# A transformer block with retention and top-k attention on one core: the last head's norm moved one block earlier and read from PSUM, and the last output weights split by converting and adding DMAs

## The chip, the cores and the metric

One NeuronCore of a Trainium2 chip runs the whole program; the other cores are idle. The metric is the device time of one execution in microseconds, median of three runs. Work is issued on five engines, each with its own queue: TensorE (PE, with its weight loads as PEld), VectorE (DVE), ScalarE (ACT), GpSimd (POOL) and SyncE (SP). DMAs are issued from SP, ACT or POOL queues.

## The reference

Layer input `h` has 16 meta tokens and 512 real ones (T = 528), width 1024, all in float32:

```
h = h + 0.5 * swiglu(rmsnorm(h), ffn1)          # width 2816
u = rmsnorm(h);  proj = u @ w_in                 # 11,848 columns: rq rk rv rg aq ak av iq ik iw g_ret g_att
yr = retention(rope(rq), rope(rk)/16, rv)        # 4 heads, dk 256, dv 512, decay per head
yr = yr * rsqrt(mean(yr*yr over dv) + eps)       # the head norm that the change moves
yr = (silu(rg) * yr) @ w_ret_out                 # 2048 x 1024: "output weights"
ya = top-k attention(rope(aq), rope(ak), av, index scores) @ w_att_out      # 8 heads, 128 keys kept
h = h + (sigmoid(g_ret) * yr + sigmoid(g_att) * ya) @ w_mix_out
h = h + 0.5 * swiglu(rmsnorm(h), ffn2);  return rmsnorm(h)
```

## The kernel before

Every float32 operand is kept as two fp32r parts, an upper one (the value rounded) and a lower one (the rest), and a product is three matmuls for each 128 x 128 weight tile: upper x upper, upper x lower, lower x upper (`mm3`). Tokens are the moving operand (512 or 2 x 264 columns), weights the stationary one.

The projections of the mixer run through one software pipeline, `steps_through` (L293). A step is (start of the load, source, product). In the block of step i it issues, in this order: the load of step i+4, the upper part of step i+2's weights, the product of step i with small jobs hung between its k tiles (`between`), the lower part of step i+2's weights, and what is to be done with the result (`behind`). Inside `manual_schedule(engines=BUSY)` PE, ACT and DVE issue in exactly the order in which the program emits them. SP and POOL are not in that list: their order is a planner's.

Raw weights land in a ring of two tiles (`raw`, 8 KB per partition each); a tile is free again when its last reader is done. The split parts lie in rings of three (`whi`, `wlo`). A step's weights are split in one of two ways: `in_two` (ACT rounds, DVE subtracts), or, for the last head's four output steps and one gate (the word "dma" in `how`), `in_two_by_dma`: ACT rounds into `whi`, ACT writes minus the rounded value into `wlo`, and a POOL DMA adds the raw tile onto `wlo` inside SBUF.

The end of the pipeline, which the change touches, runs these blocks (p = 3 is the last retention head):

- gr0 and gr1: two gates. `last_0` and `last_1` follow their products: ACT sigmoid, `weigh` (values times decayed scores, gate and squares), and in `last_1` two rounds of `pick` (`select_steps`: DVE takes the 8 largest index scores and blanks them).
- ak: keys of attention head 0. `norm_sums(p)` hangs before its k = 4: PE sums the squares, DVE scales them, POOL takes the power -0.5. `last_2`: `norm_diag` (DVE spreads the factors on a diagonal, ACT and DVE split it), then the keys' rope.
- aq: queries of head 0. `norm_all` hangs before its k = 3: two matmuls with ones spread the factors over the partitions, and ACT copies them from PSUM to SBUF (`rn`). `last_3`: `two_normed_parts` twice (DVE multiplies, ACT rounds, DVE subtracts, for the four 128-row parts of the head), then the queries' rope.
- ro0 to ro3: `outputs(p)`, four steps of the last head's output weights, 24 matmuls of 512 columns each; ro0 takes parts 0 and 1 first. Beside each: two rounds of `pick`, and DVE adds the results onto `accr`.
- gr4: a gate whose weights are split in the "dma" way; then the rest of the picks.

After the pipeline the attention stage begins: gate gr5 (`w = gr.next()`, L1948; an ordinary split, `split_w`, L117 and L118) and heads 0 to 7: scores, softmax, next head's projections, transposes. Head 0's mask for keys 128 to 255 (`bias`, L1291) comes from the last pick.

A rope (`rope_swap`) is two ACT copies that swap halves, three DVE operations, and a split.

Of the kernel before, what the change touches and what calls it, by code (L numbers as in the profile page):

```python
# [11 lines left out]
F32 = mybir.dt.float32  # L12
F32R = mybir.dt.float32r
AF = mybir.ActivationFunctionType
ALU = mybir.AluOpType
# [3 lines left out]
P = 128  # L19
D = 1024  # L20
KD = D // P
S = 512
NM = 16
T = S + NM
TX = 576
WPAD = 64
# [4 lines left out]
RH = 4  # L31
# [50 lines left out]
def kernel(ctx: ExitStack, tc: tile.TileContext, x, meta, g1, wg1, wu1, wd1, gm,  # L82
# [199 lines left out]
        nc.scalar.activation(hi, src, AF.Copy)  # L282
        return lambda: nc.vector.tensor_tensor(lo, src, hi.bitcast(F32), ALU.subtract)  # L283

    def in_two_by_dma(src, hi, lo):

        nc.scalar.activation(hi, src, AF.Copy)
        nc.scalar.activation(lo, src, AF.Copy, scale=-1.0)
        return lambda: nc.gpsimd.dma_start(lo, src, accum_op=ALU.add)

    BUSY = {mybir.EngineType.PE, mybir.EngineType.Activation, mybir.EngineType.DVE}

    def steps_through(steps):  # L293


        ws = {}

        def pre(i):
            if i < len(steps):
                steps[i][0]()  # L300

        def upper(i):
            if i < len(steps):
                v = steps[i][1]()
                n, c = v.shape[1:]
                at = (*steps[i], w_at[0])[3]
                hi, lo = (wpool.tile([P, 1024 + WPAD], F32R, tag=t, name=t, bufs=3)[:, at : at + n * c]
                          .rearrange("p (k c) -> p k c", k=n) for t in ("whi", "wlo"))
                ws[i] = (hi, lo, (in_two, in_two_by_dma)[len(steps[i]) > 4](v, hi, lo))

        def lower(i):
            if i < len(steps):
                ws[i][2]()

        for i in range(4):
            pre(i)
        for i in range(2):
            upper(i)
            yield
            lower(i)  # L320
            yield
        i = 0
        while i < len(steps):
            pre(i + 4)
            upper(i + 2)
            steps[i][2](ws.pop(i)[:2], lambda: lower(i + 2))
            yield
            i += 1
# [1025 lines left out]
    if True:  # L1354
# [152 lines left out]
        def norm_sums(h):  # L1507

            d = heads[h]
            col = sm_tile("psn")  # L1510
            for b in range(4):
                nc.tensor.matmul(col[:, b : b + 1], d["ssum"][:, b * P : (b + 1) * P], ones, start=True, stop=True)
            ms = rt.tile([P, 5], F32, tag="ms", name="ms", bufs=2)
            nc.vector.tensor_scalar(ms[:, :4], col[:, :4], 1.0 / DV, EPS, ALU.mult, ALU.add)
            r = d["rcol"] = rt.tile([P, 5], F32, tag="rcol", name="rcol", bufs=2)
            nc.gpsimd.tensor_tensor(r[:, :4], ms[:, :4], mhalf[:, :4], ALU.pow)

        def norm_diag(h):

            d = heads[h]  # L1520
            diag = tmp()[:, :S]
            d["diag"] = hi, lo = [tmp()[:, :S].bitcast(F32R) for _ in range(2)]
            TT(diag.rearrange("p (b c) -> p b c", b=4), ident.unsqueeze(1).to_broadcast([P, 4, P]),
               d["rcol"][:, :4].unsqueeze(2).to_broadcast([P, 4, P]), ALU.mult)
            return in_two(diag, hi, lo)

        def norm_all(h):

            d = heads[h]
            ps = sm_tile("psn")  # L1530
            for i, part in enumerate(d["diag"]):
                nc.tensor.matmul(ps, ones_r, part, start=i == 0, stop=i == 1)
            nc.scalar.activation(d["rn"], ps, AF.Copy)

        def normed_parts(h, c):

# [6 lines left out]
        def two_normed_parts(h, c):  # L1543
            lows = [normed_parts(h, c + i) for i in range(2)]
            for low in lows:
                low()


        raws = {}

        def tiles(key, src, c0, n, nk=KD, width=P):

            def one(i):
                def pre():
                    if i % 2 == 0:
                        m = min(2, n - i) * width
                        raws[key, i] = load_w(src[: nk * P, c0 + i * width : c0 + i * width + m], nk, m)
                return pre, lambda: raws[key, i // 2 * 2][:, :, i % 2 * width : (i % 2 + 1) * width]
            return [one(i) for i in range(n)]
# [3 lines left out]
        def pick(n):  # L1563

            for _ in range(n):
                next(picks["steps"], None)
# [5 lines left out]
        def proj(name, sl, between, behind):  # L1572

            def run(w, lower):
                if sl is None:
                    outs, ps = halves(mm_tile(name))
                else:
                    ps = sm_tile(name)
                    outs = [(ps, sl)]
                mm3(outs, w, xs, KD, between=between)  # L1580
                lower()
                behind(ps)
            return run

        def steps_of(tiles_, runs, *how):
            return [(*t, r, 0, *how) for t, r in zip(tiles_, runs)]

        THREE = ((2, pair), (4, pair), (7, pair))

# [95 lines left out]
        def outputs(h, beside):  # L1685

            def step(i):
                def run(w, lower):
                    if h == 0 and i == 0:
                        ixs.close()  # L1690
                        ap = accs.enter_context(pool("acc", 1, side="right"))
                        acc_r.extend(ap.tile([P, S], F32, tag=f"accr{c}", name=f"accr{c}") for c in range(KD))
                        vr["pool"] = vrs.enter_context(pool("vraw", 1, side="right"))
                    if i == 0:
                        if h + 1 < RH:
                            new_decay(h + 1)
                            place_tails(h + 1)
                        if h + 1 < RH:
                            heads[h + 1]["raw"] = fetch_values(h + 1, vraw())
                    pss = [sm_tile("psro") for _ in range(2)]  # L1700
                    rounds = [(j, 0, 4) for j in range(2)] if i else [(j, k, k + 2) for k in (0, 2) for j in range(2)]
                    for n, (j, k0, k1) in enumerate(rounds):
                        ps = pss[j]
                        mm3([(ps, slice(0, S))], [t[:, k0:k1, j * P : (j + 1) * P] for t in w],
                            lambda k: heads[h]["o"][k0 + k], k1 - k0, k0 == 0, True, k0 > 0)
                        if n == 0:
                            lower()
                            beside(i)
                        if k1 < 4:
                            continue  # L1710
                        a = acc_r[2 * i + j]
                        if h == 0:
                            nc.scalar.activation(a, ps, AF.Copy)
                        else:
                            TT(a, ps, a, ALU.add)
                    if i == 3 and h + 1 < RH:
                        decayed(h + 1)
                        if h + 2 == RH:
                            attention_tables()
                        values_in(h + 1)  # L1720
                return run

            how = ("dma",) if h + 1 == RH else ()
            return steps_of(tiles(("ro", h), w_ro[h * DV : (h + 1) * DV, :], 0, 4, DV // P, 2 * P),
                            [step(i) for i in range(4)], *how)

        def beside_outputs(h):
            def beside(i):
# [17 lines left out]
        def first_rope(ps, cols, n, parts):  # L1746

            y = rope_swap(ps, att["cos"][:, cols], att["sin"][:, cols], 64, n, nc.vector)
            return in_two(y, *parts)
# [13 lines left out]
        def last_1(ps):  # L1763
            keep_gate(ps)
            weigh(p, 3)
            pick(2)

        def last_2(ps):
            norm_diag(p)()
            first_rope(ps, slice(0, T), T, att["k"])()  # L1770

        def last_3(ps):
            two_normed_parts(p, 0)
            two_normed_parts(p, 2)
            first_rope(ps, REAL, S, att["q"])()

        more = gates_of(0)
# [2 lines left out]
            n = 4 - (h == p)  # L1780
            more += queries_keys(h) + gates[:n] + outputs(h - 1, beside_outputs(h - 1)) + gates[n:]
        more += steps_of(tiles("gr", w_in, OFF_GR + 2 * P, 2), [proj("psgate", REAL, (), last_0), proj("psgate", REAL, (), last_1)])
        more += steps_of(tiles("ak", w_in, OFF_AK, 1), [proj("psak", None, ((4, lambda: norm_sums(p)),), last_2)])
        more += steps_of(tiles("aq", w_in, OFF_AQ, 1), [proj("psaq", REAL, ((3, lambda: norm_all(p)),), last_3)])
        def beside_last(i):
            if i == 2:
                for c, t in enumerate(last_gates, 2):
# [1 line left out]
            pick(2)  # L1789

        more += outputs(p, beside_last)
        more += steps_of(tiles("gr4", w_in, OFF_GR + 4 * P, 1), [proj("psgate", REAL, (), first_kq.append)], "dma")
        steps += more
        with tc.manual_schedule(engines=BUSY):
            for _ in range(4):
# [486 lines left out]
```

## Time and profile before

| | |
|---|---|
| median of 3 runs | 1532.23 us (1531.75 to 1534.35) |
| profiled execution | 1531.78 us, of which its span 1530.0 us |
| PE busy | 1515.7 us, 99% of the span, 9791 matmuls |
| PEld, DVE, ACT, POOL busy | 1369.0, 1083.9, 730.8, 108.7 us |
| mean granted TensorE clock | 0.998 |
| DMA | 178.22 MB, mean 116 GB/s |

Times inside the execution count from the start of the span. "Idle before" is what an engine waited just ahead of an instruction, and the arrow names what ended the wait. A matmul's own duration overlaps its neighbours', so the pace is read from the distance between starts.

### The profile page before, as it was taken

What the parts mean: (1) busy time and instruction counts of PE and PEld (TensorE: products, weight loads), DVE (VectorE), ACT (ScalarE), POOL (GpSimd) and SP (SyncE); (2) the same over time, 40 slices, a digit from 0 to 9 for tenths busy, and PEclk for the clock granted to TensorE, in tenths of its full rate; (3) what the DMA queues carried; (4) which work ended last, traced back from release to release, by engine and by line L of the source; (5) the groups of instructions that cost most, each with busy time, mean ns of one, the idle gap of its engine ahead of it and who ended that gap; (6) DMA issues with size and microseconds to landing.
All of it is one profiled execution on the core that took longest, in us unless ns stands there. A gap on an engine that the chain in (4) does not pass through costs nothing.

```text
span 1530.0 us, 23979 instructions
## 1 busy us (share of the span) xinstructions
PE 1515.7 (99%) x9791; PEld 1369.0 (89%) x9791; DVE 1083.9 (71%) x1678; ACT 730.8 (48%) x1142; POOL 108.7 (7%) x142
## 2 busy tenths in 40 slices
PE   9999999999999999999999999999999999999998
PEld 8999999999888888788888788998888899899996
DVE  4987585776887767776858687666455788586675
ACT  6555353454354444443333447666335446254453
POOL 1000000003110120000000121111002000000000
PEclk9999999999999999999999999999999999999999
DMA  5232333326553453241312393233433322233232
GB/s 167 69 124 88 108 102 101 102 93 216 170 189 140 152 180 107 102 132 58 122 63 92 100 226 91 77 86 111 159 131 108 106 80 96 101 110 111 83 120 87
DMA packets 153390, 178.22 MB, mean 116 GB/s; under 512 B 5120, under 2 KB 124568, under 8 KB 152384
## 3 DMA queue, kind: packets, MB, share of 16 engines
q1 hardware_dynamic: 141968, 150.03, 30.2%
q0 software_dynamic: 6768, 18.20, 4.2%
q10 hardware_dynamic: 4544, 8.46, 1.6%
q8 instruction: 77, 1.26, 0.3%
q14 instruction: 33, 0.27, 0.1%
HBM read 158.04 MB, written 16.01 MB: 114 GB/s over the span
## 4 chain that ended last, share of the span: by engine, by line
PE 94%; issue 3%; DMA 1%; DVE 1%; POOL 1%; ACT 0%; POOLq 0%; ACTq 0%; SPq 0%
PE psqX L157 14%; PE psd L157 8%; PE psd L2116 8%; PE psqY L157 7%; PE psrg L157 6%; PE psro L157 4%; PE psvX L1139 4%; PE psqZ L157 3%; PE psrk L157 3%; PE psu L157 3%; PE psrq L157 3%; PE psga L157 3%; PE psmo L157 3%; PE psat L157 3%; PE psak L157 3%
## 5 line engine op out<-in xcount | busy, mean ns | idle before, releaser
L283 DVE TENSOR_TENSOR wlo<-raw,whi 128x1024 fp32r<-128x1024 f32 (+2 forms) x179 | 191.2, 1071 | 48.3 <-ACT whi L282 48.2
L282 ACT ACTIVATE whi<-raw 128x1024 fp32r<-128x1024 f32 (+2 forms) x179 | 164.5, 920 | 116.9 <-PE psd L157 37.6
L157 PE MATMUL psqX<-th,whi 128*128 128x264 f32 (+1 forms) x432 | 122.3, 283 | 0.0
L157 PE MATMUL psqX<-tl,whi 128*128 128x264 f32 (+1 forms) x432 | 122.3, 283 | 0.0
L157 PE MATMUL psqX<-th,wlo 128*128 128x264 f32 (+1 forms) x432 | 122.2, 283 | 0.0
L118 DVE TENSOR_TENSOR wlo<-raw,whi 128x1024 fp32r<-128x1024 f32 (+1 forms) x60 | 73.4, 1223 | 57.1 <-ACT whi L117 57.1
L282 ACT ACTIVATE whi<-wsum 128x1024 fp32r<-128x1024 f32 x72 | 76.3, 1060 | 70.7 <-PE psd L2116 22.0
L117 ACT ACTIVATE whi<-raw 128x1024 fp32r<-128x1024 f32 (+1 forms) x60 | 62.6, 1044 | 98.9 <-PE psat L157 26.4
L283 DVE TENSOR_TENSOR wlo<-wsum,whi 128x1024 fp32r<-128x1024 f32 x72 | 87.9, 1222 | 12.5 <-ACT whi L282 12.5
L157 PE MATMUL psro<-vo,whi 128*128 128x512 f32 x256 | 80.9, 397 | 2.9 <-ACT vo L282 2.7
L157 PEld LDWEIGHTS psqX<-th,whi 128*128 128x128 f32 x432 | 82.1, 190 | 0.1
L157 PEld LDWEIGHTS psqX<-tl,whi 128*128 128x128 f32 x432 | 82.0, 190 | 0.0
L157 PEld LDWEIGHTS psqX<-th,wlo 128*128 128x128 f32 x432 | 82.0, 190 | 0.0
L157 PE MATMUL psd<-hl,whi 128*128 128x264 f32 x352 | 71.3, 284 | 0.0
L157 PE MATMUL psd<-hh,wlo 128*128 128x264 f32 x352 | 70.7, 283 | 0.0
L157 PE MATMUL psd<-hh,whi 128*128 128x264 f32 x352 | 70.7, 282 | 0.0
L2116 PE MATMUL psd<-wlo,hh 128*128 128x512 f32 (+1 forms) x180 | 69.2, 384 | 0.0
L2116 PE MATMUL psd<-whi,hh 128*128 128x512 f32 (+1 forms) x180 | 69.2, 384 | 0.0
L2116 PE MATMUL psd<-whi,hl 128*128 128x512 f32 (+1 forms) x180 | 69.2, 384 | 0.0
L157 PEld LDWEIGHTS psro<-vo,whi 128*128 128x128 f32 x256 | 48.8, 191 | 14.7 <-ACT vo L282 3.1
L157 PEld LDWEIGHTS psd<-hh,wlo 128*128 128x128 f32 x352 | 54.4, 188 | 0.0
L157 PEld LDWEIGHTS psd<-hh,whi 128*128 128x128 f32 x352 | 54.1, 188 | 0.0
(459 smaller groups left out, 4529.1 us busy)
## 6 DMA issues: line engine op xcount, KB each, us to landing
raw<-in_ffn_w_up_dram SPq DMA_DIRECT2D x22, 1024.0 KB, 5.0
raw<-in_ffn_w_gate_dram SPq DMA_DIRECT2D x21, 1024.0 KB, 5.0
raw<-in_w_in_dram SPq DMA_DIRECT2D x19, 1024.0 KB, 5.0
raw<-in_w_in_dram SPq DMA_DIRECT2D x31, 512.0 KB, 3.5
raw<-in_ffn_w_down_dram SPq DMA_DIRECT2D x24, 512.0 KB, 4.2
w<-in_w_in_dram SPq DMA_DIRECT2D x24, 512.0 KB, 6.2
raw<-in_ffn_w_down_dram SPq DMA_DIRECT2D x12, 768.0 KB, 4.3
raw<-in_w_ret_out_dram SPq DMA_DIRECT2D x8, 1024.0 KB, 4.8
```

The costliest lines, as they stand in the source:

```text
L117: nc.scalar.activation(hi, src, AF.Copy)
L118: eng.tensor_tensor(lo, src, hi.bitcast(F32), ALU.subtract)
L157: nc.tensor.matmul(o, a[:, k, :], b[:, sl], start=first and k == 0 and i == 0, stop=last and k == nk - 1 and i == 2, skip_group_check=onto)
L282: nc.scalar.activation(hi, src, AF.Copy)
L283: return lambda: nc.vector.tensor_tensor(lo, src, hi.bitcast(F32), ALU.subtract)
L1139: nc.tensor.matmul(d[bank_][t], a, b[:, k, :], start=not onto and j + k + m == 0, stop=j + k == 3 and m == 2, skip_group_check=onto)
L2116: nc.tensor.matmul(ps, a[:, bs], m[:, j, :], start=first and i == 0, stop=last and i == 2, skip_group_check=onto)
```

## The change

Three things. First, the spread norm factors of heads 1 to 3 stay in PSUM: DVE multiplies with them there, and the ACT copy is left out (head 0 keeps it). Second, for the last head the norm's steps move up: `norm_sums` to ak's k = 3; one of the two picks of `last_1` moves into `last_2`, between the diagonal and its lower part; `norm_all` to aq's k = 1; the four normed parts from behind aq's product into it (k = 2 and k = 3); and the keys' rope from behind ak to behind aq, just ahead of the queries' rope. Third, the weights of ro0 to ro3 and gr4 come in a new way, `tiles_by_dma`: a POOL DMA loads them from DRAM and converts them to fp32r on the way (the raw tile itself is now the upper part, so `whi` isn't written), ACT writes minus that into `wlo`, and a second POOL DMA adds the same weights from DRAM.

```diff
         def upper(i):
             if i < len(steps):
                 v = steps[i][1]()
+                if isinstance(v, tuple):
+                    ws[i] = v
+                    return
...
-                ws[i] = (hi, lo, (in_two, in_two_by_dma)[len(steps[i]) > 4](v, hi, lo))
+                ws[i] = (hi, lo, in_two(v, hi, lo))
...
             for i, part in enumerate(d["diag"]):
                 nc.tensor.matmul(ps, ones_r, part, start=i == 0, stop=i == 1)
-            nc.scalar.activation(d["rn"], ps, AF.Copy)
+            if h:
+                d["rn"] = ps
+            else:
+                nc.scalar.activation(d["rn"], ps, AF.Copy)
...
+        def tiles_by_dma(src, c0, n, nk=KD, width=P):
+            raws_ = {}
+            def one(i):
+                def rows(c, m):
+                    return src[: nk * P, c0 + c : c0 + c + m].rearrange("(k p) c -> p k c", p=P)
+                def pre():
+                    if i % 2 == 0:
+                        m = min(2, n - i) * width
+                        raw = wpool.tile([P, 2048], F32, tag="raw", name="raw", bufs=2)
+                        raws_[i] = raw[:, : nk * m].bitcast(F32R).rearrange("p (k c) -> p k c", k=nk)
+                        nc.gpsimd.dma_start(raws_[i], rows(i * width, m))
+                def parts():
+                    hi = raws_[i // 2 * 2][:, :, i % 2 * width : (i % 2 + 1) * width]
+                    lo = wpool.tile([P, 1024 + WPAD], F32R, tag="wlo", name="wlo", bufs=3)[:, : nk * width]
+                    lo = lo.rearrange("p (k c) -> p k c", k=nk)
+                    nc.scalar.activation(lo, hi.bitcast(F32), AF.Copy, scale=-1.0)
+                    return hi, lo, lambda: nc.gpsimd.dma_start(lo, rows(i * width, width), accum_op=ALU.add)
+                return pre, parts
+            return [one(i) for i in range(n)]
...
         def last_1(ps):
             keep_gate(ps)
             weigh(p, 3)
-            pick(2)
+            pick(1)
         def last_2(ps):
-            norm_diag(p)()
-            first_rope(ps, slice(0, T), T, att["k"])()
+            first_kq.append(ps)
+            low = norm_diag(p)
+            pick(1)
+            low()
         def last_3(ps):
-            two_normed_parts(p, 0)
-            two_normed_parts(p, 2)
+            first_rope(first_kq.pop(), slice(0, T), T, att["k"])()
             first_rope(ps, REAL, S, att["q"])()
...
-        more += steps_of(tiles("ak", w_in, OFF_AK, 1), [proj("psak", None, ((4, lambda: norm_sums(p)),), last_2)])
-        more += steps_of(tiles("aq", w_in, OFF_AQ, 1), [proj("psaq", REAL, ((3, lambda: norm_all(p)),), last_3)])
+        more += steps_of(tiles("ak", w_in, OFF_AK, 1), [proj("psak", None, ((3, lambda: norm_sums(p)),), last_2)])
+        more += steps_of(tiles("aq", w_in, OFF_AQ, 1), [proj("psaq", REAL, ((1, lambda: norm_all(p)), (2, lambda: two_normed_parts(p, 0)),
+                                                                                  (3, lambda: two_normed_parts(p, 2))), last_3)])
...
-        more += steps_of(tiles("gr4", w_in, OFF_GR + 4 * P, 1), [proj("psgate", REAL, (), first_kq.append)], "dma")
+        more += steps_of(tiles_by_dma(w_in, OFF_GR + 4 * P, 1), [proj("psgate", REAL, (), first_kq.append)])
```

In `outputs` the last head takes `tiles_by_dma(w, 0, 4, DV // P, 2 * P)` in place of `tiles(("ro", h), ...)` in the same way: one load for ro0 and ro1, one for ro2 and ro3.

## Rows read from the trace of the kernel before

**Rows 1.** PE's waits over the whole span: total us, times, longest us.
```profile
PE psro L157 <- ACT vo L282: 2.7, 1, 2.7
PE psS L1907 <- ACT gate L1340: 1.1, 1, 1.1
```
**Rows 2.** PE in order of time, aq to gr4: start, us, instruction, idle before.
```profile
859.14 0.40 PE L157 MATMUL psaq<-xh,whi 128*128 128x512 f32 x1
...
861.22 0.62 PE L1532 MATMUL psn<-tmp,ones_r 128*128 128x512 f32 x2
...
864.87 0.39 PE L157 MATMUL psaq<-xh,wlo 128*128 128x512 f32 x1
...
867.94 0.50 PE L157 MATMUL psro<-vo,whi 128*128 128x512 f32 x1 [2.68 <-ACT vo L282]
...
882.30 0.50 PE L157 MATMUL psro<-vo,wlo 128*128 128x512 f32 x1 [0.55 <-DMA wlo<-raw]
...
892.95 0.39 PE L157 MATMUL psgate<-xh,whi 128*128 128x512 f32 x1
```
**Rows 3.** The chain that ended last: head 0's output steps; the last head's sums.
```profile
645.99 21.97 PE psro L157 x96
...
855.51 0.79 PE psn L1512 x8
```
**Rows 4.** Two stretches: us, PE, PEld, DVE, ACT, POOL busy, granted clock, DMA.
```profile
868.00:873.00 5.00, 4.78 (x13) 3.56 (x14) 4.38 (x8) 2.91 (x5) 0.00 (x0) 0.66 0.74 120
928.00:930.00 2.00, 0.87 (x7) 0.67 (x6) 1.70 (x5) 1.97 (x3) 0.43 (x1) 1.00 0.02 5
```
**Rows 5.** DVE in order of time, from the norm's sums to the queries' rope.
```profile
855.83 0.56 DVE L1288 MAX8 top<-score 128x8 f32<-128x384 f32 x1
...
856.97 0.15 DVE L1514 TENSOR_SCALAR ms<-psn 128x4 f32<-128x4 f32 x1
...
859.99 0.69 DVE L283 TENSOR_TENSOR tmp<-tmp 128x512 fp32r<-128x512 f32 x1 [0.70 <-ACT tmp L282]
861.24 0.71 DVE L1252 TENSOR_TENSOR tmp<-psak,cos 128x528 f32<-128x528 f32 x1 [0.56 <-ACT tmp L1251]
...
864.02 0.71 DVE L283 TENSOR_TENSOR akq<-tmp,akq 128x528 fp32r<-128x528 f32 x1 [0.71 <-ACT akq L282]
866.53 1.30 DVE L1538 TENSOR_TENSOR to<-to,three 128x512 f32<-128x512 f32 x2 [1.81 <-ACT three L1533]
...
870.52 1.29 DVE L283 TENSOR_TENSOR vo<-to,vo 128x512 fp32r<-128x512 f32 x2
872.34 0.69 DVE L1252 TENSOR_TENSOR tmp<-psaq,cos 128x512 f32<-128x512 f32 x1 [0.53 <-ACT tmp L1251]
...
875.05 0.69 DVE L283 TENSOR_TENSOR akq<-tmp,akq 128x512 fp32r<-128x512 f32 x1 [0.70 <-ACT akq L282]
```
**Rows 6.** POOL in order of time.
```profile
856.14 1.35 POOL L289 DMA_DIRECT2D wlo<-raw  x1 [65.57 <-ACT wlo L288]
857.28 1.29 POOL L1516 TENSOR_TENSOR rcol<-ms,mhalf 128x4 f32<-128x4 f32 x1
...
877.21 1.27 POOL L289 DMA_DIRECT2D wlo<-raw  x1 [9.72 <-ACT wlo L288]
```
**Rows 7.** ACT in order of time: the minus copy of ro2.
```profile
875.87 1.04 ACT L288 ACTIVATE wlo<-raw 128x1024 fp32r<-128x1024 f32 x1
```
**Rows 8.** Landing times, 850 to 900 (`wlo`), 850 to 960 (`vo`: converting and adding, 1 MB).
```profile
DMA to landing us min/median/max: 5.0/5.1/6.2
...
DMA to landing us min/median/max: 6.6/8.3/10.1
```
**Rows 9.** The chain that ended last, 850 to 955: gr5's load.
```profile
885.42 5.10 DMA raw<-in_w_in_dram
```
**Rows 10.** DVE in the attention stage's first microseconds.
```profile
891.72 1.23 DVE L118 TENSOR_TENSOR wlo<-raw,whi 128x1024 fp32r<-128x1024 f32 x1 [3.04 <-ACT whi L117]
...
912.83 0.29 DVE L1291 TENSOR_SCALAR bias<-score 128x256 f32<-128x256 f32 x1
```

More of the change, by code (lines that the diff above doesn't have):

```diff
@@ L283, in in_two @@
         return lambda: nc.vector.tensor_tensor(lo, src, hi.bitcast(F32), ALU.subtract)
[L285 to L289, printed above, removed]
     BUSY = {mybir.EngineType.PE, mybir.EngineType.Activation, mybir.EngineType.DVE}
@@ L1583, in proj, with steps_of @@
             return run
-        def steps_of(tiles_, runs, *how):
-            return [(*t, r, 0, *how) for t, r in zip(tiles_, runs)]
+        def steps_of(tiles_, runs):
+            return [(*t, r, 0) for t, r in zip(tiles_, runs)]
         THREE = ((2, pair), (4, pair), (7, pair))
@@ L1721, in step @@
                 return run
-            how = ("dma",) if h + 1 == RH else ()
-            return steps_of(tiles(("ro", h), w_ro[h * DV : (h + 1) * DV, :], 0, 4, DV // P, 2 * P),
-                            [step(i) for i in range(4)], *how)
+            w = w_ro[h * DV : (h + 1) * DV, :]
+            ts = tiles_by_dma(w, 0, 4, DV // P, 2 * P) if h + 1 == RH else tiles(("ro", h), w, 0, 4, DV // P, 2 * P)
+            return steps_of(ts, [step(i) for i in range(4)])
         def beside_outputs(h):
```

## The prediction

> **What bounds the kernel now.** I read the page first: PE is busy 99% of the span, so only what PE waits for, or runs at a lower clock, can be won. The list of PE's waits comes next. Its two long entries lie at the seam between the retention heads and attention: 2.7 us before the last head's output product, ended by ACT's split of the normed parts, and 1.1 us in head 1's scores [rows 1]. The other entries that name an output product, 0.5 and 0.2 us, lie in ro2 and ro0 too, none with heads 0 to 2, so the copies that heads 1 and 2 lose were not waited for.
>
> PE's timeline through the seam gives what is to be won [rows 2]. From the last start in aq (864.87) to the first in gr4 (892.95) are 28.08 us. The same 96 matmuls took 21.97 us for head 0 [rows 3], a pace of 0.23 us; with one such step the stretch needs 22.2 us. So 5.9 us are lost: about 2.8 in the gap before ro0, 0.55 in front of ro2's lower weights, and the rest after the gap, where the granted clock over 868 to 873 was 0.66 and the matmuls took twice as long (1.2 GHz for 2.4). The 1.1 us gap at 928 left the clock at 1.00 [rows 4].
>
> The DVE timeline says why the gap is there. The norm's sums (ms) stand behind two picks at 856.97; the keys' rope runs from 861.24 to 864.73, the normed parts only from 866.53 to 871.81, and the queries' rope from 872.34 to 875.74 [rows 5]. ACT's copy of the factors stood in its queue behind that first rope, and its end at 866.5 released the parts.
>
> **The change, step by step, on the clock of the old trace.**
>
> *Sums.* The second pick, which moves, starts at 855.83; ms can take its place, 1.14 us sooner, since the products that it reads (855.51 to 856.30) move forward by a k tile too [rows 3, 5]. POOL then needs 1.29 us for the power, and shares its queue with ro0's adding DMA (1.35 us), now ready earlier by one ACT copy of 1.05 [rows 6, 7]. I take the factors at 857.7, not 858.57.
>
> *Diagonal.* Diagonal and upper part took 1.4 us from 858.57 to 859.99; the lower part adds 0.69 [rows 5, 6]. The moved pick (some 1.2 us) now covers the upper part's 0.7 and overruns it by 0.5. Result at 860.2 instead of 860.7.
>
> *Spreading.* At k = 1 of aq PE stands at 859.14 + 3 x 0.23 = 859.83. It is in order, so it waits about 0.4 us there: a new wait, with the rest of aq queued behind it. At k = 3 it had waited for nothing.
>
> *Normed parts.* The two spreading matmuls take 0.62 us [rows 2], so DVE can start at 860.95 with the operand in PSUM. That form is not in the trace; DVE's products with a PSUM operand (psaq x cos, 512 columns) take 0.69, the pairs from SBUF 1.30 for two, so I charge nothing. The four parts took 5.28 us and end at 866.2. Ro0, which starts at 865.5 with parts 0 and 1 (done at 863.6), does not wait: the 2.8 us gap and the half clock are gone. If the cover fails, they come back.
>
> *Ropes.* Now two in a row behind the parts: 3.49 + 3.40 us, to 873.1 (875.74 before) [rows 5]. Head 0's scores need them only after gr5. But ACT's minus copy for ro2 is emitted behind the queries' rope, so it ends at 873.3 (1.04 us [rows 7]), and ro2's adding DMA can be issued at 873.6, against 877.21 [rows 6].
>
> *Ro2, late next.* Ro0 and ro1 now run 865.5 to 876.5; ro2's third matmul, the first to need the lower part, stands at 876.95. Adding DMAs of this size landed 5.0 to 6.2 us after issue [rows 8]. Their source was SBUF; from DRAM only one of twice the size is shown, landing within 10.1, so the bounds are 5.0 and 10.1. I take 5.05, the nearest rows: 878.65, a wait of 1.7 us. After 2.7 us the clock had fallen, after 1.1 it had not; I assume it holds. The Trainium skill ("DMA: Bandwidth & Descriptors", section "Anatomy of one DMA — SWDGE (gpsimd) path") fits such DMAs with 2.0 us plus bytes at 436 GB/s. By that an estimate for 512 KB is 3.2 us, and ro2 would not wait at all; the trace disagrees for adding DMAs, with 5.0 as its shortest.
>
> *Loads on POOL.* Two 1 MB loads leave SP for POOL, with conversion. The nearest rows are 6.6 to 10.1 us for `vo`, in a busier stretch [rows 8]. Ro0's would be issued at 841 and is first read at 853.8: hidden up to 12 us. Ro2's has longer. No charge.
>
> *Raw ring.* The raw tile is now an operand of the product and is freed by it. Gr4's load must wait for ro1's last matmul, 876.5 (SP issued it at 871.4 before). Issue and landing 5.9 us, ACT 1.05, adding DMA 5.1 and queueing: lower part at about 889.5. Ro3 ends at 889.2 and the third matmul stands at 889.65: 0 to 2 us of wait, I take 0.3. Gr5's load likewise waits for the end of ro3, 889.2; it was issued at 885.42 and took 5.1 us [rows 9]. With the same 5.1, ACT 1.05 and DVE 1.23 its lower part is there at 896.7, with a load 1.5 us quicker than in that contended moment at 895.2; gr4 ends at 895. Wait 0 to 2 us, I take 0.5.
>
> *DVE and head 0.* From 893 on DVE was full, and the last pick ended at 912.83, having lost 3.04 us in front of gr5's split [rows 10]. DVE now comes out of the ropes 2.6 us sooner, so the mask comes at least about as much sooner as PE does, and I let the 1.1 us wait at 928 shrink by 0.4.
>
> *ACT* saves five copies of 1.05 us and three shorter ones; it was not the bound, and what that brings is in the times above.
>
> **Sum.** Won: 5.9 + 0.4 = 6.3. New waits: 0.4 + 1.7 + 0.3 + 0.5 = 2.9. Net 3.4 us off the span of 1530.0, so 1528.4 for an execution like the profiled one (1531.78), and 1528.8 against the median 1532.23, which is 0.45 above it. A difference of 0.2% (3.06 us) is about what can be told from none; this forecast lies just beyond it.
>
> **Rivals.**
>
> *All hidden.* Ro2's lower part lands in time, or only by a fraction late, and both raw tiles come back soon enough. Then only 0.4 of the new waits stays: 5.9 us less, 1526.3. For it: ACT is free in this stretch and nothing else is on the queue when ro2's DMA is issued. Against: 5.0 us is the shortest of five landings.
>
> *The wait moves to ro2.* Reading DRAM while adding takes 7 us instead of 5, ro2 waits 3.6, and after such a gap the clock halves again (some 2 us): 3.9 of the 3.4 won are gone, 1532.7. For it: the longest landings of [rows 8] are DRAM ones. Against: these carried 1 MB. The Trainium skill ("SBUF — State Buffer", section "Who interferes with whom") adds a way to such a delay: a DVE instruction in a 2-port mode keeps GpSimd from writing descriptors. Its candidates here are the masks of 0.3 us [rows 10], so by it a landing would slip 0.3 us and no more; no row here shows it.
>
> *POOL's order.* Gr4's load now stands on POOL, where it waits for ro1's end; before, it waited on SP and blocked nobody. In the program's text it comes ahead of ro2's adding DMA. If the planner keeps that order, ro2's DMA goes out at 876.5 plus 1.3 to 1.9 us of issue, behind a 512 KB load on the same queue, and lands at about 884. PE then stands from 876.95 to 884, 7 us instead of 1.7, and pays the half clock again (2): 7.3 us more than the forecast, 1536.1, slower. It decides as soon as the load goes first. Against: POOL's order isn't the text's. The adding DMA of ro0, emitted after the power, ran before it at 856.14, when it was ready first [rows 6]; here ro2's is ready 3 us sooner than the load. That margin is not wide for a planner's costs.
>
> *Without effect.* The norm isn't ready sooner because the sums wait on something else than the pick: the gap at ro0 and its half clock return (5.1 of the 6.3 us won), ro2's wait goes, the other new waits (1.2) stay: 1532.2, as before.
>
> **How the numbers follow.** Forecast 0.45 (its own range 1526.8 to 1530.8; six tenths of it beyond 0.2%), all hidden 0.18, wait moved to ro2 0.16, POOL's order 0.14, without effect 0.07. Faster: 0.27 + 0.18 + 0.01 = 0.46. Slower: POOL's order and the worst of the moved wait, 0.14 + 0.03 = 0.17. Same: 0.37. The range leaves out a tenth on each side: 1525.8, all hidden with a little more from head 1's wait, to 1534.5, between the moved wait and POOL's order.
>
> **What would show it.** Right: the clock at 1.00 from 865 to 876, ro0 without a wait, one short PE wait at the spreading and one of 1 to 2.5 us on `wlo` in ro2, loads of `raw` on POOL behind the products. Wrong: a wait of over 4 us in front of ro2 with the load ahead of the adding DMA; a clock below 1 after ro2; landings over 6 us for 512 KB from DRAM; or a head 0 that gives back what the seam won, with DVE waiting for gr5's weights among the picks.

## The result, and the profile after

The change made the kernel slower: 1542.28 us (median of 6 runs, 1539.57 to 1542.87) against 1533.07 for the kernel before beside it (6 runs, 1531.75 to 1534.35), ratio 1.0056 with a 95% interval of 1.0045 to 1.0066. The forecast was 1528.8, its range 1525.8 to 1534.5. The profiled execution has a span of 1540.8 us, 10.8 more than before. Lines have moved: 1571 is the adding DMA, 1564 the converting load, 1943 and 1950 are the scaling and the transposing of the probabilities (1916 and 1923 before). The traces are not aligned: ak, the first block that the change touches, starts at 852.38 us in the kernel before, at 852.67 in the changed kernel, and between 852.34 and 853.70 in the runs further down. A comparison of two positions to better than that has to count from ak's start.

PE's waits between 840 and 1000, total us, times, longest; they answer to [rows 1]:
```profile
PE psPT L1950 <- DVE pj L1943: 7.4, 2, 5.9
PE psro L157 <- DMA wlo<-in_w_ret_out_dram: 2.7, 1, 2.7
PE psgate L157 <- DMA wlo<-in_w_in_dram: 1.6, 1, 1.6
PE psro L157 <- DVE accr L1740: 0.5, 1, 0.5
```
The two waits of [rows 1] are gone. In their place stand ro2's lower weights, gr4's, and one that was nowhere before: head 0's transposes wait 7.4 us for the probabilities.

PE in order of time, against [rows 2], and below it the same place in the kernel before:
```profile
860.35 0.63 PE L1529 MATMUL psn<-tmp,ones_r 128*128 128x512 f32 x2
...
865.62 0.63 PE L157 MATMUL psro<-vo,raw 128*128 128x512 f32 x2
...
880.75 0.50 PE L157 MATMUL psro<-vo,wlo 128*128 128x512 f32 x1 [2.73 <-DMA wlo<-in_w_ret_out_dram]
...
892.98 0.40 PE L157 MATMUL psgate<-xh,raw 128*128 128x512 f32 x1
...
895.21 0.50 PE L157 MATMUL psgate<-xh,wlo 128*128 128x512 f32 x1 [1.61 <-DMA wlo<-in_w_in_dram]
...
925.29 0.90 PE L1950 MATMUL psPT<-ident,pj 128*128 128x128 f32 x3 [5.88 <-DVE pj L1943]
927.67 2.39 PE L1950 MATMUL psPT<-ident,pj 128*128 128x128 f32 x10 [1.48 <-DVE pj L1943]
...
929.93 0.78 PE L157 MATMUL psgate<-xh,whi 128*128 128x512 f32 x1
```
```profile
917.10 1.58 PE L1923 MATMUL psPT<-ident,pj 128*128 128x128 f32 x13
...
918.54 0.48 PE L157 MATMUL psgate<-xh,whi 128*128 128x512 f32 x1
```
Ro0 starts 2.3 us sooner and without a wait. But gr4 starts where it did, 892.98 against 892.95 [rows 2]: all but 0.3 us of what the seam had won (counted from ak) is gone by then. The transposes, which before began at 917.10 without a wait, begin 8.2 us later; the gate behind them (gr6) 11.4 us later.

Stretches of the changed kernel, columns as in [rows 4], then one of the kernel before:
```profile
880.00:885.00 5.00, 4.25 (x12) 3.42 (x13) 4.90 (x13) 0.00 (x0) 0.00 (x0) 0.68 1.24 217
...
893.00:917.00 24.00, 22.39 (x118) 18.87 (x117) 18.42 (x52) 11.24 (x13) 5.49 (x13) 1.00 1.10 276
...
925.00:934.00 9.00, 7.23 (x26) 5.91 (x27) 7.83 (x15) 5.84 (x12) 2.60 (x2) 0.55 0.44 117
```
```profile
893.00:917.00 24.00, 24.00 (x136) 21.15 (x135) 22.29 (x71) 13.03 (x20) 5.57 (x13) 1.00 0.97 245
```
The clock halved behind the 2.73 us gap, as it had in [rows 4] behind one of 2.68, and again behind the 5.88 us; not behind the 1.61. And DVE, busy 22.3 of the 24 us from 893 to 917 before, was busy only 18.4: it waited.

For what, ACT's timeline shows, first the changed kernel's, then that of the kernel before:
```profile
912.24 0.63 ACT L1940 ACTIVATE pj<-tmp,stat 128x400 f32<-128x400 f32 x1
...
915.34 1.06 ACT L117 ACTIVATE whi<-raw 128x1024 fp32r<-128x1024 f32 x1 [2.38 <-DMA raw<-in_w_in_dram]
921.81 1.06 ACT L117 ACTIVATE whi<-raw 128x1024 fp32r<-128x1024 f32 x1 [5.41 <-DMA raw<-in_w_in_dram]
922.77 0.51 ACT L1940 ACTIVATE pj<-tmp,stat 128x272 f32<-128x272 f32 x1
```
```profile
914.04 0.52 ACT L1913 ACTIVATE pj<-tmp,stat 128x272 f32<-128x272 f32 x1 [3.27 <-DVE stat L1912]
...
917.05 1.04 ACT L117 ACTIVATE whi<-raw 128x1024 fp32r<-128x1024 f32 x1
```
`pj` are head 0's four exponentials, `whi` the splits of the next weights. The heads lie behind the `manual_schedule` block, so the order on ACT and DVE is the planner's here. Before, these splits came behind the exponentials and found their weights landed. Now two of them (gr6's and those of head 2's queries) stand ahead of the last three, and ACT waits in front of both: 2.38 us, then 5.41 us for weights that PE uses only from 941. DVE has the same order. On it the mask and the last probabilities end:
```profile
914.29 0.29 DVE L1288 TENSOR_SCALAR bias<-score 128x256 f32<-128x256 f32 x1
916.43 1.22 DVE L118 TENSOR_TENSOR wlo<-raw,whi 128x1024 fp32r<-128x1024 f32 x1 [1.85 <-ACT whi L117]
...
922.90 1.22 DVE L118 TENSOR_TENSOR wlo<-raw,whi 128x1024 fp32r<-128x1024 f32 x1 [3.90 <-ACT whi L117]
...
927.13 0.49 DVE L1943 TENSOR_SCALAR pj<-pj,stat 128x528 f32<-128x528 f32 x1
```
```profile
916.75 0.50 DVE L1916 TENSOR_SCALAR pj<-pj,stat 128x528 f32<-128x528 f32 x1
```
The second fence is the kernel before. The mask is 1.5 us later than in [rows 10], the last probabilities 10.

The loads themselves, in SP's queue, first the changed kernel's, then the second and the fifth of the kernel before:
```profile
892.99 0.37 SPq L133 DMA_DIRECT2D raw<-in_w_in_dram  x1
900.34 0.99 SPq L133 DMA_DIRECT2D raw<-in_w_in_dram  x2
908.34 0.37 SPq L133 DMA_DIRECT2D raw<-in_w_in_dram  x1
909.83 0.37 SPq L133 DMA_DIRECT2D raw<-in_w_in_dram  x1
```
```profile
888.75 0.37 SPq L133 DMA_DIRECT2D raw<-in_w_in_dram  x1
...
902.94 0.37 SPq L133 DMA_DIRECT2D raw<-in_w_in_dram  x1
```
Gr5's load goes out when ro3's last matmul has read the raw tile (892.98), the next two when gr4's has (900.3). Before, gr5's went out at 885.42 [rows 9] and the next at 888.75. The fifth, for head 2's queries, went out 6.9 us later than before, and it also landed after 11.9 us instead of 3.9, beside gr6's load (908.34) and two 1 MB loads of values (904.20 and 911.22). So it is 14.9 us late, and more than half of that is the slower landing. No run takes this half away by itself.

### The profile page after: what moved, and what is told of

It reads as the page before. It is cut to its first block, busy times and chain, and to the rows that moved or that the text cites. A ratio compares the mean times of both kernels' runs of the same rounds, so it can differ in the third digit from the quotient of the medians.

```text
span 1540.8 us, 23962 instructions
## 1 busy us (share of the span) xinstructions
PE 1518.9 (99%) x9791; PEld 1370.8 (89%) x9791; DVE 1084.0 (70%) x1678; ACT 724.3 (47%) x1134; POOL 111.6 (7%) x145
## 4 chain that ended last, share of the span: by engine, by line
PE 92%; DVE 3%; issue 3%; DMA 1%; POOL 1%; ACT 0%; POOLq 0%; ACTq 0%; DVEq 0%
PE psqX L157 13%; PE psd L2143 8%; PE psd L157 7%; PE psqY L157 7%; PE psrg L157 6%; PE psvX L1136 4%; PE psro L157 4%; PE psqZ L157 3%; PE psrk L157 3%; PE psu L157 3%; PE psrq L157 3%; PE psga L157 3%; PE psmo L157 3%; PE psat L157 3%; PE psak L157 3%
## 5 line engine op out<-in xcount | busy, mean ns | idle before, releaser
L157 PE MATMUL psro<-vo,whi 128*128 128x512 f32 x192 | 59.6, 391 | 0.2 <-DVE accr L1740 0.2
L157 PEld LDWEIGHTS psd<-hl,whi 128*128 128x128 f32 x352 | 53.9, 188 | 0.0
```

The source lines that it names most:

```text
L157: nc.tensor.matmul(o, a[:, k, :], b[:, sl], start=first and k == 0 and i == 0, stop=last and k == nk - 1 and i == 2, skip_group_check=onto)
```

## The experiments

Each ran beside the kernel before on the same chip; ratios are to it.

**Which half costs.** The norm's part alone, and the DMAs' part alone:
```
e1:  - ts = tiles_by_dma(w, 0, 4, ...) if h + 1 == RH else tiles(...)     (gr4 alike)
     + how = ("dma",) if h + 1 == RH else ()
e2:  the kernel before, with tiles_by_dma for ro0 to ro3 and gr4
```


> The changed kernel with ro0 to ro3 and gr4 back on the old way (SP load, two ACT copies, adding DMA from the raw tile), so the norm's part of the change alone. Theory A (the raw tiles, held until the product's end, delay the attention weights and with them head 0): gr5's load is issued at about 885 again, not 893; PE does not wait at psPT; the gap before ro0 is gone; time 1527 to 1530. Theory B (two ropes in a row and the moved pick push DVE's picks back, and so head 0): PE still waits over 4 us for the probabilities at psPT, time 1538 or more.

Measured: 1530.76 us, ratio 0.9983 (0.9974 to 0.9992), just above the range of theory A. Gr5's load is back at 883.46, no wait at the transposes. PE's waits in this run:
```profile
PE psro L157 <- DMA wlo<-raw: 2.7, 1, 2.7
PE psS L1940 <- ACT gate L1343: 0.8, 1, 0.8
```


> The kernel before with only the converting and adding DMAs for ro0 to ro3 and gr4. Theory A: the gap before ro0 stays (5 us lost there), gr5's load is issued at ro3's end, about 893, ACT has a weight split that waits for its load ahead of head 0's exponentials, and PE waits 4 to 8 us at psPT; time 1538 to 1546. Theory B: no wait at psPT, time 1531 to 1534.

Measured: 1541.74, ratio 1.0050 (1.0038 to 1.0062), gr4 waiting 3.0 us, and at the transposes:
```profile
PE psPT L1945 <- DVE pj L1938: 5.0, 2, 3.5
```
Theory B falls: the whole loss comes with the DMAs' part. Here ACT stands at other weights, those of head 1's keys, ahead of the first exponential: their load took 10.5 us and ACT waits 5.98 us for it. But e1 falls short of the 5.9 us too, since ro2's wait is there without any DMA from DRAM: gr4 starts at 892.91, as before. By the profiled executions its gain of 0.17% arises behind gr6; it was not followed further.

**Which tiles.**
```
e3:   gr4 back: steps_of(tiles("gr4", ...), [...], "dma")
e10:  steps_of(tiles_by_dma(w, 0, 2, ...), runs[:2]) + steps_of(tiles(.., w, 4 * P, 2, ..), runs[2:], "dma"), gr4 back
```


> The changed kernel with gr4 alone back on the old way (its raw tile is then freed by its adding DMA and not by its product, 900.3). Theory A: the load behind gr5's goes out at about 893.5 instead of 900.3, the splits of head 0 come 5 us sooner, the wait at psPT shrinks from 7.4 us to under 2, gr4's own wait of 1.6 us goes: 1531 to 1536. Theory C (loads and adding DMAs that read DRAM are slow in themselves, the ring does not matter): only gr4's own wait goes, about 1540.5, with psPT still over 5 us.

Measured: 1537.05, ratio 1.0024 (1.0014 to 1.0033): loads at 890.95 and 893.6, gr4's wait gone, and at the transposes:
```profile
PE psPT L1956 <- DVE pj L1949: 3.3, 2, 1.8
```
4.9 of the 8.6 us come back (1.0056 to 1.0024), against nearly 2 by theory C. The time is 1 us above theory A's range and the wait more than the 2 us that I allowed, as one split (head 2's queries) still stood ahead of the last exponentials.

> The changed kernel with the converting and adding DMAs for ro0 and ro1 alone; ro2, ro3 and gr4 on the old way. Ring theory: the raw tiles that were held into the attention stage are those of ro2 and ro3 and of gr4; without them gr5's load goes out at about 885 again and head 0 has no wait at psPT: 1529.5 to 1532, that is all of the loss is gone though two loads and two adding DMAs still come from DRAM. Theory C (DMAs that convert or read DRAM cost time in themselves): over 1533.

Measured: 1537.48, ratio 1.0027 (1.0016 to 1.0037): by the number theory C's, and outside the ring theory's forecast. By the trace there is no wait at the transposes, as the ring theory has it, but:
```profile
PE psro L157 <- DMA wlo<-raw: 5.6, 1, 5.6
PE psS L1943 <- ACT gate L1343: 1.1, 1, 1.1
```
Gr4's load, held by ro1's raw tile, goes out on SP at 877.15 instead of 867.03 in e1, and meets ro2's adding DMA, issued at 876.26: that lands after 7.9 us instead of 5.0. A load that nobody waits for came at the wrong moment. That the meeting costs the time is argued, not shown: in e8 below a load issued 1.6 us behind ro2's adding DMA left it at 5.8 us, while ro3's, issued between two loads, took 9.5 (5.8 in e1). From ak's start e10 has lost 2.4 us at gr4, the same 2.4 at gr6, and 1.7 more by the end, which this doesn't account for.

**The order on ACT and DVE.** Loads as in the changed kernel (the fifth out at 909.8, landing after 11.1 us), the two splits bound to the last exponential, shortened:
```
+ nc.vector.tensor_scalar(one, m[:, 2:3], 0.0, 1.0, ALU.mult, ALU.add)     # m: the exponential's sum
- split(v, hv, lv, eng)
+ nc.scalar.activation(hv, v, AF.Identity, scale=one)
+ eng.tensor_tensor(lv, v, hv.bitcast(F32), ALU.subtract)
```


> The changed kernel in which the two weight splits that stood on ACT ahead of head 0's last three exponentials (those of gr6 and of head 2's queries) take as their scale a column of ones that DVE computes from the last exponential's sum, so that no order can put them ahead; loads as in the changed kernel. Theory A1 (the loss in head 0 is the in-order queue: ACT and DVE stand at weights that nobody needs yet): the 7.4 us at psPT shrink to under 1.5 and the half clock behind it goes; the waits at ro2 and gr4 stay; time 1530 to 1534. Theory A2 (the weights are so late that their products wait anyway): the wait moves to gr6's product or to head 1's scores, time 1538 or more.

Measured: 1535.49, ratio 1.0012 (1.0003 to 1.0020); no wait at the transposes, no half clock behind them:
```profile
919.22 1.58 PE L1959 MATMUL psPT<-ident,pj 128*128 128x128 f32 x13
```
So 6.7 of the 8.6 us (1.0056 to 1.0012) come back by the order alone, with the weights as late as ever. I had asked for 1534 at most: the late weights still cost half a microsecond each at head 1's queries and at gr6.

**The source of an adding DMA.**
```
- nc.gpsimd.dma_start(lo, src, accum_op=ALU.add)
+ nc.gpsimd.dma_start(lo, <the same columns of w_ro or w_in in DRAM>, accum_op=ALU.add)
```


> As e1, the norm's part alone, with the adding DMAs of ro0 to ro3 and gr4 reading the weights from DRAM instead of the raw tile in SBUF; SP's loads and both ACT copies stay, and the raw tile is freed by the second copy. If the source costs little, ro2's lower part lands 5.1 us after its issue as in e1, with a wait of 2.7 us. If reading DRAM while adding is slower, it lands 5.9 us or more after it and ro2 waits 3.5. The ring theory says that head 0 stays without a wait at psPT in either case; time 1530 to 1532.

Measured: 1531.37, ratio 0.9992 (0.9984 to 1.0001), no wait at the transposes; ro2 waits 3.49 us instead of e1's 2.73, with the DMA issued at 875.66 and 875.59 and landing after 5.8 and 5.0 us. DRAM costs 0.8 us for 512 KB. The Trainium skill ("DMA: Bandwidth & Descriptors", section "Anatomy of one DMA — SWDGE (gpsimd) path") gives by its fit an estimate of 3.2 us; both sources disagree, at 5.0 and 5.8.

**Reading PSUM alone.** The kernel before, with `d["rn"] = ps` for heads 1 to 3.

> The kernel before with only the factors of heads 1 to 3 read from PSUM, without the copies on ACT. Heads 1 and 2 were not waited for, so nothing there. In the last head the copy's end released the normed parts at 866.5, but the first rope held DVE until 865.4: the parts can start 1 us sooner, the gap before ro0 shrinks from 2.7 to under 2 us, and the half clock behind it may go. Theory: 0 to 3 us faster, 1530.5 to 1533.5. Rival (the copy was hidden by the rope): unchanged gap, 1533.6.

Measured: 1531.78, ratio 0.9992 (0.9983 to 1.0001). The gap before ro0 shrinks to 1.18 us and no half clock follows, but ro2's lower weights are then waited for, 2.13 us instead of 0.55. Ak starts 1.3 us later here than in the kernel before (853.65), gr4 0.2 us sooner (892.73): the seam has won 1.5 us, and 1.3 of them are still there at gr6 (918.48). The time, 1.2 us less, fits, with an interval that just takes in no change.

**What the seam is worth.** All on e1, shortened. E6 moves both ropes behind ro2's split; e7 is e6 without 5 of the 16 picks of the mask's last group, so it computes another mask and only tells what DVE's time is worth; e9 moves the queries' rope alone; e12 puts picks between the ropes; e11 is e12 with four products on POOL:
```
e6:   last_3: no rope;         beside_last(0): + first_rope(keys) + first_rope(queries), pick(2)
e9:   last_3: keys' rope;      beside_last(0): + first_rope(queries), no pick; beside_last(1): pick(4)
e12:  last_3: keys' rope, pick(2);  beside_last(0): + first_rope(queries), no pick
e11:  e12, with nc.gpsimd.tensor_tensor(acc_r[c], acc_r[c], gate, ALU.mult) for c = 2 to 5
```


> As e1, the norm's part alone, with both ropes moved from behind aq's product into ro0's, behind the two ACT copies and the adding DMA of ro2. Both theories: ro2's adding DMA is issued at about 868 instead of 875.6, the 2.7 us wait at ro2 and the half clock behind it go, and gr4 starts at about 888.5 instead of 892.9. Theory P (PE is the bound): 4 us come off the end, about 1526.5. Theory D (DVE's picks, which ended 1 us ahead of psPT in e1, bound head 0): PE waits 3 to 6 us for the probabilities at psPT, and the time is that of e1 or worse, 1530 to 1534.

> As e6, with 5 of the 16 picks of the mask's last finished group left out (the mask is then another one; some 4.9 us of DVE less). Theory D: the wait at psPT goes, PE keeps what the seam won, 1525 to 1528, and 2 us or more under the run with ropes behind ro2's split. Theory P: no difference to that run.

E6: 1532.76, ratio 0.9998 (0.9989 to 1.0007). Ro2's lower weights are in time (DMA at 867.83), yet PE waits as long in front of ro2, now for DVE, whose additions stand behind both ropes and free the PSUM. Gr4 starts at 891.89 and not at 888.5, and the transposes wait. E7: 1528.80, ratio 0.9972 (0.9962 to 0.9982). PE at the transposes, e6 first, then e7:
```profile
916.33 0.55 PE L1958 MATMUL psPT<-ident,pj 128*128 128x128 f32 x3
918.72 1.31 PE L1958 MATMUL psPT<-ident,pj 128*128 128x128 f32 x10 [1.84 <-DVE pj L1951]
```
```profile
916.39 1.58 PE L1958 MATMUL psPT<-ident,pj 128*128 128x128 f32 x13
```
PE arrives at the same time, within 0.3 us counted from ak, and e7 goes on without the wait: theory D. The spans of the two profiled executions differ by 2.0 us (1529.1 and 1527.1). By the medians e7 is 4 us ahead; e6's profiled execution was its fastest, and what the others lost more is not in a trace. In front of ro2 both have the same gap of 2.56 us, up to 879.25 and 879.58. The stretch behind it, e6 first, then e7:
```profile
879.00:883.00 4.00, 3.75 (x10) 3.00 (x11) 3.90 (x10) 0.28 (x1) 0.87 (x1) 0.57 1.06 179
```
```profile
879.00:883.00 4.00, 3.42 (x15) 2.83 (x16) 3.90 (x9) 0.62 (x1) 1.15 (x2) 1.00 0.97 160
```
The clock fell in e6 and not in e7. But e7 then waits 1.33 us for DVE in front of gr4, which starts at 892.19, so that little of this is left at the transposes.

> As e1, the norm's part alone, with the keys' rope where it was behind aq, the queries' rope behind ro2's two copies and adding DMA, and ro0's two picks done beside ro1. Ro2's adding DMA is issued at about 871.8 and lands by 877; DVE still has one rope ahead of ro0's additions, which end at about 877.6 and free ro2's PSUM, so PE waits at most 1.2 us there and the clock stays at 1.00: gr4 starts at 889 to 890.5 instead of 892.9. Theory D (DVE's picks bound head 0, with 1 us to spare in e1): 2 to 3 us of it come back as a wait at psPT, time 1529 to 1531. Theory P (they don't): 1527 to 1528.

E9: 1532.12, ratio 0.9993 (0.9984 to 1.0002), above both theories. The output steps wait 0.6 us in all; gr4 then waits 2.85 for DVE, which had idled 2.41 us between the ropes and was behind with its additions, the clock falls to 0.76 over the 7 us behind it, and the mask comes at 915.40.

> As e1, the norm's part alone, with ro0's two picks between the ropes: keys' rope, picks, then ro2's copies on ACT and the queries' rope, which finds its operands ready. DVE loses no time between the ropes (in the run with the queries' rope moved without the picks it stood idle for 4 us between 868 and 876), ro2's adding DMA is issued at about 872, PE waits at most 1.2 us in ro2, gr4 starts at 889 to 890.5. Theory D (DVE bounds head 0 from the mask on): the mask ends at 911.7 as in e1, the probabilities at 916, and PE waits 2 to 2.5 us for them: time that of e1 less 1, 1529 to 1531. Theory P: 1527 to 1528.

E12: 1532.79, ratio 0.9999 (0.9990 to 1.0009), above both theories again. The seam is now what the prediction promised: from aq to gr4 one wait of 0.2 us, the clock at 1.00, gr4 at 887.55, 5.4 us sooner than before. And nothing of it arrives. The chain that ended last, up to head 1's queries:
```profile
889.04 10.52 DMA raw<-in_w_in_dram
...
899.67 0.04 ACT whi L117
...
902.65 0.61 ACT gate L1989
903.25 0.04 issue
903.30 1.89 PE psaq L157 x7
```
The retention heads' memory came free sooner, so the first 1 MB loads of values went out at 888.78 and 890.90 (894.21 and 896.32 in the changed kernel), on top of the 512 KB of weights issued at 889.04, which took 10.52 us. ACT stood at their split, with two splits of values and gr4's gate behind it. PE's waits:
```profile
PE psPT L1960 <- DVE pj L1953: 3.7, 2, 1.9
PE psaq L157 <- ACT gate L1989: 2.7, 1, 2.7
```

> As the run with the picks between the ropes, with the four products of accumulators and gates (gates 2 to 5) on POOL instead of DVE, 2.6 us of DVE less ahead of the mask. Theory D: the probabilities are ready 2 to 2.6 us sooner, the wait at psPT goes, and the time is 1526.5 to 1528.5, 2 us under the run without this. Theory P: no difference between the two.

E11: 1530.35, ratio 0.9982 (0.9974 to 0.9991), some 2.6 us under e12; no wait at the transposes, but the 2.4 us at head 1's queries stay, and with them the time is 2 us above its forecast. With e1 it is the version that computes the same and beats the kernel before, by 0.17 to 0.18%.

How much sooner than in the kernel before PE reaches gr4 and gr6, in us, both counted from ak's start:

| run | gr4 | gr6, behind head 0's transposes |
|---|---|---|
| changed kernel | 0.3 | -11.1 |
| e1 | 0.2 | 0.2 |
| e4 | 1.5 | 1.3 |
| e6 | 1.3 | -1.1 |
| e7 (another mask) | 1.3 | 1.3 |
| e9 | 1.7 | -1.0 |
| e12 | 5.4 | -2.5 |
| e11 | 5.3 | 1.2 |

## Why the prediction was wrong

*Sums to ro0:* right. Factors 857.87 (857.7 forecast), diagonal 860.32 (860.2), parts 861.01 to 866.28 (860.95 to 866.2); ro0 doesn't wait. The 0.4 us at the spreading did not show: aq itself starts 0.5 later, 0.3 of it from ahead of ak.

*Ropes and ro2:* right in kind, three terms too small. The ropes end at 874.25, not 873.1: I added only DVE's busy spans, and each rope waits 0.5 us more for ACT's halves. Ro2's adding DMA went out at 874.77 and landed after 5.9 us, not 5.05. The wait became 2.73, not 1.7, and my assumption that the clock holds failed with it: 0.68 over 5 us costs 1.6. These and DVE's 0.5 leave next to nothing of the seam's gain, which is why gr4 starts at 892.98. The rival "the wait moves to ro2" is close to what happened here, with 5.9 us for its 7 and 2.73 for its 3.6.

*POOL's order:* the rival did not come. Ro2's DMA at 874.77 went ahead of gr4's load at 877.11.

*Raw ring:* the mechanism was right, and I followed it for two loads. Gr4's load landed 9.2 us after its issue, behind two adding DMAs on its queue, not 5.9; its lower part came at 895.2, a wait of 1.6. Gr5's load went out at ro3's end as forecast, and PE did not wait for it.

*DVE and head 0:* this is the step that failed. I let the mask come "at least about as much sooner as PE does" and put a gain of 0.4 us here. Measured are 7.4 us of wait at head 0's transposes and a clock of 0.55 over the 9 us from 925: gr6 is 11.1 us later, counted from ak. Each later load waits for a raw tile in its turn, so the whole sequence from gr5's load on slipped by 7 to 12 us (888.75 to 900.34 for the second), the fifth landed slowly on top of that, and the engines that split those weights also hold head 0's exponentials. I had the list of what is queued behind a late weight for PE, not for ACT and DVE. E1 and e2 show that the loss comes with the DMAs' part, e3 and e10 that head 0's wait shrinks and goes as fewer tiles are held, e5 that most of the loss is the order on ACT and DVE. Why the planner wrote that order was not tested: e6, e9 and e12, with no tile held, have one split ahead too, but its weights had landed. My signs of being wrong had a head 0 that gives back what the seam won, but with gr5's weights; the clock below 1 behind ro2 and landings over 6 us for 512 KB from DRAM (6.2, 7.0 and 6.8) came as well.

*The 5.9 us* were not to be had in full, either: e12 and e11 won 5.4 and 5.3 of them at gr4 and had lost 2.5 and kept 1.2 at gr6. Before, the last probabilities ended at 917.25, just as PE arrived (917.10), so a gain at the seam had no slack to land in. E7 and e11 show that DVE's time holds part of it back; the late load in e12 and e11 is in the chain shown above, but no run takes it away.

## What to carry to other kernels

When a load's buffer becomes an operand, list every later load of the ring, when it now starts, which engine splits it, and what else stands in that engine's queue; the first wait on PE is not the end of it. Before crediting a gain at a seam, look at the next place where PE meets another engine: a start with no wait and no slack there gives the gain back. And a buffer that comes free sooner starts its transfer sooner, which can fall on top of one that is being waited for. When two traces are compared, take out first what they differ by ahead of the change.

## What the runs showed of the hardware

- The length of a gap on PE did not by itself decide the clock behind it. Over the 4 us behind the gap the granted clock was 0.58 after 2.56 us in e6, 1.00 after 2.56 us in e7, 1.00 after 2.67 us in e12 (up to 903.30), 1.00 after 1.18 and 2.13 us in e4, but 0.73 after 1.46 us in e2 (up to 867.66).
- An adding DMA of 512 KB, with no load of another queue issued around it, landed 5.0 to 5.1 us after its issue from SBUF (e1, the first three) and 5.9 from DRAM (e2, the first two). With a 512 KB load of SP's queue 0.9 us behind it, it took 7.9 (e10). A plain 512 KB load took 10.5 us in e12, issued between two 1 MB converting loads (888.78 and 890.90), against 3.4 to 5.2 in the kernel before (884 to 905), which has such loads too, from 894.18 on.
- ACT waits at a late operand with ready work behind it: of the 5.41 us here, the last 3.5, since the next exponential's operands were there at 918.31. The Trainium skill ("TensorE: Matmul & The Clock Gate", the table at its head) calls the queues of ScalarE and VectorE strictly first in, first out; the trace agrees.
